# Another order of the mixer's projections: compressed keys, values and gates first, three query quarters last

## The chip, the cores and the metric

The kernel runs on one core of a Trainium2 chip. The metric is the device time of one launch in microseconds (us); lower is better. Before the change the median of three runs is 2270.88 us (2266.21 to 2273.49).

## The reference, cut to what matters

The program computes three transformer layers over 512 tokens of width 1024 in fp32. The change lies in the third layer, the mixer. It normalises x, projects it once with `w_in`, and splits the result:

```python
z = rms_norm_2(x, mix_norm_g) @ w_in
(nq, kc, vc, ks_, vs_, kw, vw, ng, cu, gq, gk, gv, ga, gr) = jnp.split(z, split_at, axis=-1)
kc, vc = compress_kv(kc, ...), compress_kv(vc, ...)       # blocks of 32 tokens through a small MLP
y_nsa  = nsa_attention(nq, kc, vc, ks_, vs_, kw, vw, sigmoid(ng), rel_bias)   # 8 heads of 64
y_conv = conformer_conv(cu, ...)                           # GLU, causal depthwise conv of 31, layer norm
o      = gla_chunked(gq, gk, gv, log_a)                    # 8 chunks of 64, a state carried from one to the next
y_gla  = rms_norm_2(o, ...) * silu(gr)
x = x + concatenate([y_nsa, y_conv, y_gla]) @ w_out
```

A feed-forward layer (called f2 below) follows.

## The kernel before

**Matmuls.** Every weight is split into a high and a low fp32r part (`weight`, line 370): a DMA on the SP queue into `wr` (2 buffers), a scaled copy on ACT into `wh`, a scaled difference on DVE into `wl` (4 buffers each). A product is then three fp32r matmuls (`mm3`, line 287). Line numbers of profile rows are mostly those of these helpers: 285 is every matmul, 295 every transpose, 148 every DVE, ACT or POOL instruction, so rows are told apart by tile.

**Order of work.** The program is written by Python threads (generators) that a small planner (`Order`, line 76) interleaves. Of the threads that can go on, the one with the lowest rank is taken; a thread yields a flag to wait for, or a time worked out from planned costs (`due`, `sleep`). Nothing of this exists on the chip: there the engines run their queues in order and wait on semaphores. The framework below may move an instruction ahead of its place where its operands and buffers are free.

**The mixer** (`mixer`, line 1378). One thread of rank 1, `project` (line 1505), runs ten projections in the order of the string `MIX_ORDER` (line 34):

- `conv`: 512 columns in two token halves; starts the 31-tap convolution (`conformer1`, rank 0, DVE), later `conformer2`.
- `b`: gla's values and gate ranks (400 columns, by token). `a`: attention's values and gates `gate`, and half of gla's output gate `gr` (408 columns, by token). When `a` ends, the flag `gates` is set.
- `gla`: gla's queries and keys (2 tiles of 128 columns); starts the thread `gla` (line 1752, rank 0). That thread waits for `gates` (line 1813) before it applies `gr`, then runs four token steps, each with two state updates (tiles `diag`, `gst`, `gA`, `gs`), and sets `done_c`.
- `k`: selected and window keys (2 tiles). `kv`: keys and values to be compressed (2 tiles); starts two `compress` threads (line 1603, rank 0) whose matmuls are `s<-Xp,w`.
- `q0` to `q3`: a quarter of the queries each (1 tile, two heads).

Each tile of 128 columns costs 8 x 3 matmuls of 512 columns. After the last projection the flag `made` is set. A thread `begin` (line 1511) waits for both compressions, the keys and `q0`, and sets `first`. Only then are the attention threads added: four of `lane` (line 1523, rank 0), for quarters t = 0 and 1 and their two heads e; each goes on with quarter t + 2. A lane waits for its own quarter `fq[t]` and, for t of 2 and 3, for `made`; the first lane of a quarter loads the bias tile `T` (`nsa_bias`, line 1589); then `nsa_c` scores the compressed keys (`s<-kch`), and `nsa` (line 1707) goes through four query tiles of growing length. When both heads of a quarter are done, the result is split into X, which needs `made`, since the projections read X.

Three threads of lower rank bring dense matmuls of 512 columns: `others` (line 1550, rank 1), which multiplies the conv and gla parts by `w_out` after `made`, `done_c` and `done_y`; `out(0)` after quarters 0 and 1; `out(1)` after quarters 2 and 3.

```python
MIX_ORDER = "conv b gla k q0 kv a q1 q2 q3"          # line 34
def begin():
    yield from self.wait(*cmp, ready, fq[0])
    first.done = True
```

Of the kernel before, what the change touches and what calls it, by code (L numbers as in the profile page):

```python
# [30 lines left out]
CONV_GAP = 1000.0  # L31
LAT = 200.0
FAC = 1.0
MIX_ORDER = "conv b gla k q0 kv a q1 q2 q3"
SL = 1.0
D = 1024
EPS = 1e-6
# [147 lines left out]
class Model:  # L185
# [1192 lines left out]
    def mixer(self, x, nxt):  # L1378
# [4 lines left out]
        with self.phase("mx") as pp:  # L1383
# [22 lines left out]
            made, done_c, done_v, done_y, done = fl(), fl(), fl(), fl(), fl()  # L1406
# [30 lines left out]
            fq, qs = [fl() for _ in range(4)], Slots(3)  # L1437

            def query(t):

                yield from (qs if t < 3 else self.xs).take()
                parts = [(lambda r, e=e: r.rearrange("p (k e d) -> p k e d", e=2, d=64)[:, :, e, :],
                          W[:, e * 256 + t * 64:e * 256 + t * 64 + 64].rearrange("(k p) d -> p k d", p=P))
                         for e in range(2)]
                yield from self.wu.take()
                units = [self.weight(1024, parts, [gm[:, k:k + 1] for k in range(8)])]

                qT[t] = (pp.tile([P, 2, S], F32R, name=self.uid("nq"), tag="nq", bufs=3) if t < 3 else
                         self.sc.tile([P, 2, S], F32R, name=self.uid("nq"), tag="xn"))
                yield from self.gemm_feat(x, units, P, [blk(0)], lambda j, ps: self.split_halves(qT[t], ps, 0.125))  # L1450
                fq[t].done = True

            with self.phase("mxc") as pc:
# [51 lines left out]
                def project():  # L1505
                    for job in MIX_ORDER.split():
                        yield from query(int(job[1])) if job[0] == "q" else {
                            "a": proj_a, "b": proj_b, "conv": proj_conv, "gla": proj_gla, "k": proj_k, "kv": proj_kv}[job]()
                    made.done = True
# [5 lines left out]
                ready, gates = fl(), fl()  # L1515
# [4 lines left out]
            with self.phase("mxn") as pn:  # L1520
                head, left, fy, fo = {}, [2] * 4, [fl() for _ in range(4)], [fl(), fl()]

                def lane(t0, e):
                    for t in (t0, t0 + 2):
                        yield from self.wait(fq[t], *([made] if t >= 2 else []))
                        if t not in head:
                            hd = head[t] = [fl()]
                            yield from heads.take()
                            yield from self.acc.take()
                            hd += [self.ptile("acc"), [], *self.nsa_bias(pn, t)]  # L1530
                            hd[0].done = True
                        yield from self.wait(head[t][0])
                        T2, cB = head[t][3:]
                        yield from self.cr.take()
                        yield from self.bank("s")
                        sc = self.nsa_c(pn, t, e, qT[t], kc, cB, gate)
                        ready = fl()
                        od.add(self.nsa_cv(sc, self.padded(vals[:, 8], e), head[t][1:3], ready), 0)
                        for qt in range(NT):
                            yield from self.nsa(pn, t, e, qt, qT[t], kh, kl, vals, T2, gate, head[t][1:3], ready)  # L1540
                        left[t] -= 1
                        if left[t] == 0:
                            (qs if t < 3 else self.xs).give()
                            heads.give()
                            yield from self.wait(made)
                            self.split(*[y[:, t, :] for y in self.X], head[t][1])
                            self.acc.give()
                            fy[t].done = True

                def others():  # L1550
                    yield from self.wait(made, done_c)
                    for t in range(NT):
                        ts = slice(t * P, (t + 1) * P)
                        yield from self.bank("tr")
                        self.split(*[y[:, 6:, ts] for y in self.X], self.transpose(gr[:, t, :], 2))
                        yield
                    yield from self.wait(done_y)
                    for c in range(2):
                        yield from self.gemm_tok(lambda k, t: self.x_at(4 + k, t), 4, [(Wo[512:, :], c * 512, 512)],
                                                 self.add_h(c * 512), lambda t: [])  # L1560
                    fo[0].done = True

                def unit(k0, m, pieces):
                    c0, parts = pieces[0][1], []
                    for e in range(2):
                        parts.append((lambda r, e=e: r.rearrange("p (a w) -> p a w", w=512)[e * 64:(e + 1) * 64],
                                      Wo[e * 256 + k0 * 64:e * 256 + (k0 + m) * 64, c0:c0 + 512]
                                      .rearrange("(a p) n -> p a n", p=64)))
                    return self.weight(m * 512, parts)

                def out(g):

                    yield from self.wait(*fy[2 * g:2 * g + 2], *fo[:g * 2])
                    token = nxt()[1] if g else lambda t: None
                    yield from self.gemm_rows(lambda k, t: self.x_at(2 * g + k, t), 2,
                                              lambda c, k0: unit(2 * g + k0, 2, [(Wo, c * 512, 512)]),
                                              lambda t: [], token)
                    (fo[1], done)[g].done = True

                self.nw, heads = Slots(2), Slots(2)  # L1580
                for t in range(2):
                    for e in range(2):
                        od.add(lane(t, e), 0)
                od.add(others(), 1)
                od.add(out(0), 2)
                od.add(out(1), 2)
                od.run(done)
# [397 lines left out]
```

## Time and profile before

| | |
|---|---|
| median of three runs | 2270.88 us (2266.21 to 2273.49) |
| the profiled execution's own time | 2270.06 us |
| its span from first to last instruction | 2268.3 us |
| mean granted TensorE clock | 0.988 of full speed |
| TensorE (PE) matmul busy | 2197.4 us, 97% |
| TensorE weight loads (PEld) | 1861.9 us, 82% |
| VectorE (DVE), ScalarE (ACT), GpSimd (POOL) | 1336.6, 1062.0, 173.0 us |
| the mixer's matmuls | from about 1534 to about 1831 us |

Times in the trace count from the span's start. The time of a launch is the span and about 2 us around it. Matmuls are pipelined and their ends are modelled, so that matmuls that come one by one can look like a busy engine: the number of starts in a stretch and the granted clock (1.00 is 2.4 GHz, 0.50 is 1.2 GHz) have to be read beside the busy time.

### The profile page before, as it was taken

Reading aid. Unit: us, or ns where it says so; the run is one execution under the profiler, and the core shown is the slowest. Engines: PE = TensorE matmul, PEld = TensorE weight load, DVE = VectorE, ACT = ScalarE, POOL = GpSimd, SP = SyncE. Lnnn points to the kernel's source line nnn. Section 1 sums busy time; section 2 is a strip of 40 time slices with the busy share of each in tenths; the row PEclk is TensorE's granted clock in tenths of the full one; section 3 lists DMA queues with packets and bytes.
Section 4 is the critical chain, followed back from the end, with each engine's and each line's share of the span. In section 5 each row is a group of like instructions: output and inputs, shape, how many; then the busy total and the mean of one; then the engine's idle time right before and its main releaser. Section 6 shows DMA issues by size and latency. Waiting matters only on the chain.

```text
span 2268.3 us, 30282 instructions
## 1 busy us (share of the span) xinstructions
PE 2197.4 (97%) x11166; PEld 1861.9 (82%) x11166; DVE 1336.6 (59%) x2885; ACT 1062.0 (47%) x2102; POOL 173.0 (8%) x232
## 2 busy tenths in 40 slices
PE   7987999999999999999999999999999999999998
PEld 5866798888887888888988888889978888888886
DVE  6668656446545777767565366357977643333344
ACT  4547445334444565555454254254657543323333
POOL 3123000000001121210000000001010000000000
PEclk9999999999999999999999999999989999999999
DMA  6323123332332412212133233234430123323322
GB/s 190 99 63 93 59 84 98 103 98 84 107 98 80 128 43 59 68 40 82 54 107 102 94 103 97 79 98 122 99 91 22 54 66 101 99 91 99 99 89 82
DMA packets 168839, 200.01 MB, mean 88 GB/s; under 512 B 19201, under 2 KB 123709, under 8 KB 168688
## 3 DMA queue, kind: packets, MB, share of 16 engines
q1 hardware_dynamic: 165172, 194.77, 28.1%
q10 hardware_dynamic: 2940, 2.02, 0.3%
q0 software_dynamic: 576, 1.26, 0.3%
q8 instruction: 88, 1.44, 0.3%
q14 instruction: 63, 0.52, 0.1%
HBM read 195.87 MB, written 7.38 MB: 90 GB/s over the span
## 4 chain that ended last, share of the span: by engine, by line
PE 91%; DVE 4%; ACT 1%; DMA 1%; issue 1%; POOL 0%; DVEq 0%; POOLq 0%; SPq 0%; ACTq 0%
PE acc L285 82%; PE s L285 4%; PE tr L295 4%; PE tr L285 1%; DVE wl L148 1%; DVE sb L148 1%; PE s L295 0%; DVE ss L148 0%; DVE X L148 0%; ACT wh L148 0%; DMA xn<-biasB 0%; DVE qs L148 0%; ACT wT L148 0%; DVE qn L148 0%; DMA tb<-rel_bias 0%
## 5 line engine op out<-in xcount | busy, mean ns | idle before, releaser
L285 PE MATMUL acc<-X,wh 128*128 128x512 f32 (+1 forms) x2592 | 734.9, 370 | 4.0 <-DVE X L148 4.0
L285 PEld LDWEIGHTS acc<-X,wh 128*128 128x128 f32 x2592 | 469.9, 189 | 85.0 <-DVE X L148 4.7
L285 PE MATMUL acc<-wh,X 128*128 128x512 f32 (+4 forms) x1664 | 502.0, 380 | 0.2 <-DVE X L148 0.2
L285 PE MATMUL acc<-X,wl 128*128 128x512 f32 (+1 forms) x1296 | 474.7, 369 | 0.0
L148 ACT ACTIVATE wh<-wr,gcol 128x512 fp32r<-128x512 f32 (+5 forms) x480 | 289.6, 656 | 208.4 <-PE acc L285 123.8
L148 DVE SCALAR_TENSOR_TENSOR wl<-wr,gcol,wh 128x512 fp32r<-128x512 f32 (+5 forms) x480 | 306.1, 674 | 131.5 <-ACT wh L148 129.5
L285 PEld LDWEIGHTS acc<-wh,X 128*128 128x128 f32 x1664 | 309.9, 190 | 45.9 <-DVE X L148 0.7
L285 PE MATMUL acc<-wl,X 128*128 128x512 f32 (+4 forms) x832 | 322.4, 388 | 7.3 <-DVE qn L148 3.3
L285 PEld LDWEIGHTS acc<-X,wl 128*128 128x128 f32 x1296 | 244.2, 189 | 40.8
L148 DVE TENSOR_TENSOR wl<-wr,wh 128x1024 fp32r<-128x1024 f32 (+1 forms) x134 | 152.5, 1144 | 183.8 <-ACT wh L148 183.6
L148 POOL TENSOR_TENSOR ss<-ss,mhalf 128x1 f32<-128x1 f32 (+3 forms) x140 | 128.9, 923 | 1727.4 <-DVE ss L148 1703.0
L148 ACT ACTIVATE wh<-wr 128x1024 fp32r<-128x1024 f32 (+1 forms) x134 | 132.5, 995 | 238.9 <-PE acc L285 191.2
L285 PE MATMUL acc<-wh,hh 128*128 128x512 f32 x528 | 205.7, 390 | 0.0
L285 PE MATMUL acc<-wl,hh 128*128 128x512 f32 x528 | 204.5, 389 | 0.0
L285 PE MATMUL acc<-wh,hl 128*128 128x512 f32 x528 | 203.7, 390 | 0.0
L285 PEld LDWEIGHTS acc<-wl,X 128*128 128x128 f32 x832 | 158.1, 190 | 32.8 <-DVE qn L148 3.6
L148 DVE SCALAR_TENSOR_TENSOR cv<-acc,cw,cv 128x511 f32<-128x511 f32 (+1 forms) x176 | 126.1, 745 | 95.2 <-ACT cv L148 94.4
L148 DVE TENSOR_TENSOR h<-h,acc 128x512 f32<-128x512 f32 x120 | 81.6, 684 | 61.3 <-PE acc L285 60.8
L285 PEld LDWEIGHTS acc<-wl,hh 128*128 128x128 f32 x528 | 99.1, 188 | 20.5
L285 PEld LDWEIGHTS acc<-wh,hl 128*128 128x128 f32 x528 | 99.1, 188 | 20.4
L285 PEld LDWEIGHTS acc<-wh,hh 128*128 128x128 f32 x528 | 99.1, 188 | 20.4
L148 ACT ACTIVATE wT<-tr 128x128 f32<-128x128 f32 (+3 forms) x160 | 68.8, 435 | 91.4 <-PE tr L295 90.6
(312 smaller groups left out, 2688.5 us busy)
## 6 DMA issues: line engine op xcount, KB each, us to landing
wr<-ffn_w_in SPq DMA_DIRECT2D x160, 256.0 KB
wr<-ffn_w_out SPq DMA_DIRECT2D x40, 512.0 KB
wr<-ple_w_gate SPq DMA_DIRECT2D x24, 512.0 KB
wr<-ffn_w_gate SPq DMA_DIRECT2D x40, 256.0 KB
wr<-ffn_w_up SPq DMA_DIRECT2D x40, 256.0 KB
wr<-ffn_w_down SPq DMA_DIRECT2D x20, 512.0 KB
wr<-a_w_qkv SPq DMA_DIRECT2D x32, 256.0 KB
wr<-b_w_o SPq DMA_DIRECT2D x16, 512.0 KB
```

Source lines behind the costliest of these rows:

```text
L148: return fn(*args, **kw)
L285: self.nc.tensor.matmul(out, lhsT=a, rhs=b, start=start, stop=stop)
L295: self.nc.tensor.transpose(out, src, self.ident[:src.shape[0], :src.shape[0]])
```

## The change

`MIX_ORDER` is another string, and a lane also waits for the flag `gates`. Nothing is added to or taken from what is computed.

```diff
-MIX_ORDER = "conv b gla k q0 kv a q1 q2 q3"
+MIX_ORDER = "conv kv a b k q0 gla q1 q2 q3"
...
                 def lane(t0, e):
                     for t in (t0, t0 + 2):
-                        yield from self.wait(fq[t], *([made] if t >= 2 else []))
+                        yield from self.wait(fq[t], gates, *([made] if t >= 2 else []))
```

## Rows read from the trace of the kernel before

**Rows 1.** Mixer by stretch: us, busy us and starts of PE PEld DVE ACT POOL, clock.
```profile
1562.00:1674.00 112.00, 112.00 (x618) 100.12 (x618) 98.18 (x199) 67.91 (x158) 5.97 (x11) 1.00 0.47 125
1674.00:1710.00 36.00, 32.09 (x157) 24.37 (x155) 29.38 (x137) 23.18 (x83) 2.61 (x4) 0.81 0.06 16
1710.00:1822.00 112.00, 111.19 (x751) 99.31 (x749) 73.33 (x262) 70.47 (x192) 1.61 (x2) 1.00 0.15 41
```

**Rows 2.** The same view and columns, shorter stretches.
```profile
1674.00:1684.00 10.00, 7.99 (x52) 6.71 (x51) 9.59 (x44) 8.16 (x24) 1.29 (x2) 0.94 0.21 53
1684.00:1698.00 14.00, 12.98 (x45) 9.44 (x43) 9.30 (x48) 5.00 (x20) 1.32 (x2) 0.56 0.00 1
1698.00:1710.00 12.00, 11.12 (x62) 8.22 (x62) 10.49 (x48) 10.02 (x40) 0.00 (x0) 1.00 0.00 1
1740.00:1750.00 10.00, 10.00 (x86) 9.73 (x86) 6.73 (x34) 7.58 (x23) 0.00 (x0) 1.00 0.00 0
1770.00:1780.00 10.00, 10.00 (x88) 9.82 (x87) 7.99 (x33) 6.78 (x20) 0.00 (x0) 1.00 0.01 2
```

**Rows 3.** Lanes by tile: min/median/max ns, first and last start.
```profile
L285 PE MATMUL s<-kch,nq x32: 178/263/1015, 1674.2 to 1778.8; 128*128 128x32 f32 x32
...
L285 PEld LDWEIGHTS s<-nkh,nq x64: 186/190/337, 1677.3 to 1812.5; 128*128 128x128 f32 x64
```

**Rows 4.** ACT in order of time, 1605 to 1680 us.
```profile
1622.05 0.59 ACT L148 ACTIVATE gk<-tr 64x512 f32<-64x512 f32 x1
...
1642.85 1.06 ACT L148 ACTIVATE gr<-gr 128x1024 f32<-128x1024 f32 x1
...
1671.62 0.58 ACT L148 ACTIVATE nq<-acc 64x512 fp32r<-64x512 f32 x1
```

**Rows 5.** Waits of PE, 1672 to 1712 us: total, times, longest.
```profile
PE acc L285 <- DVE gst L148: 1.5, 3, 0.9
...
PE s L285 <- DVE nm L148: 1.0, 2, 0.7
```

**Rows 6.** The gla thread by tile, the same columns.
```profile
L285 PE MATMUL acc<-gst,gq x16: 379/380/634, 1651.0 to 1707.7; 128*128 128x256 f32 x16
L148 ACT ACTIVATE gq<-acc x2: 379/382/384, 1581.9 to 1582.2; 128x256 f32<-128x256 f32 x2
...
L285 PE MATMUL tr<-diag,gs x8: 592/674/1201, 1650.1 to 1703.5; 128*128 128x512 f32 x8
```

**Rows 7.** Dense matmuls with `w_out`, by line, 1710 to 1822 us.
```profile
L285 PE MATMUL acc<-wh,X 128*128 128x512 f32 x102 | 32.9, 395 | 0.0
...
L285 PE MATMUL acc<-wl,X 128*128 128x512 f32 x51 | 21.0, 411 | 0.0
```

**Rows 8.** PE in order of time: dense matmuls of a query projection.
```profile
1667.92 0.62 PE L285 MATMUL acc<-X,wh 128*128 128x512 f32 x2
1668.37 0.39 PE L285 MATMUL acc<-X,wl 128*128 128x512 f32 x1
1668.60 0.62 PE L285 MATMUL acc<-X,wh 128*128 128x512 f32 x2
```

**Rows 9.** Compression, by tile.
```profile
L285 PE MATMUL s<-Xp,w x128: 215/275/275, 1627.9 to 1667.0; 128*128 128x62 f32 x128
```

**Rows 10.** Weight splits and table loads, by line, 1562 to 1710 us.
```profile
L148 DVE SCALAR_TENSOR_TENSOR wl<-wr,gcol,wh 128x256 fp32r<-128x256 f32 x24 | 10.4, 480 | 0.2 <-ACT wh L148 0.2
...
L148 DVE SCALAR_TENSOR_TENSOR wl<-wr,gcol,wh 128x128 fp32r<-128x128 f32 x32 | 9.4, 345 | 0.6 <-ACT wh L148 0.6
...
L148 ACT ACT_TABLE_LOAD x6 | 7.7, 1283 | 0.1
```

**Rows 11.** SP's queue in order of time; the bias tile's first readers, by tile.
```profile
1633.46 5.63 SPq L1630 DMA_DIRECT2D w<-cmp_w_v  x2
...
1665.49 1.10 SPq L1593 DMA_DIRECT2D T<-rowsC  x2
...
L148 DVE COPY cB<-T x16: 162/186/218, 1676.9 to 1753.3; 128x62 f32<-128x62 f32 x4, 128x46 f32<-128x46 f32 x4, 128x30 f32<-128x30 f32 x4, 128x14 f32<-128x14 f32 x4
```

## The prediction

> **What bounds the kernel now.** I read the page first: PE is nearly always busy and holds most of the chain of waits. No stretch can gain much, unless PE's busy time there is not what it seems. The next view, busy time by stretch, shows such a place. In the mixer's projections, from 1562 to 1674 us, PE is busy without a gap at full clock, although DVE is near its limit as well; from 1710 to 1822 us, attention beside the output projection, it is nearly so [rows 1]. In the 36 us between, PE is idle for 36 - 32.09 = 3.91 us, runs at a mean clock of 0.81, and starts 157 matmuls, 4.36 per us, where the stretch behind it starts 751 in 112 us, 6.71 per us [rows 1]. The shorter stretches show how: from 1674 to 1684 us PE works 7.99 of 10 us, and then the granted clock falls to a mean of 0.56 for 14 us, which is mostly the level of 1.2 GHz [rows 2].
>
> This is attention's start. The first lane scores start at 1674.2 us [rows 3]. The last query projection has just ended: its result is copied at 1671.62 us [rows 4]. So all four lanes start on their smallest tiles, where each matmul waits for a reduction or for gla's state update [rows 5], and no dense matmul is left to fill in: the `w_out` products wait for gla's end, and gla's last state matmul starts at 1707.7 us [rows 6]. Only behind 1710 us do 102 + 51 dense matmuls stand between attention's [rows 7]. Later stretches that hold hardly any of these, 1740 to 1750 and 1770 to 1780 us, have PE busy all the time at full clock [rows 2]: lanes on long tiles fill PE by themselves.
>
> **The change part by part.** *The recoverable loss.* Idle time is 3.91 us, the clock's loss is 36 x (1 - 0.81) = 6.84 us; together 10.75 us [rows 1]. Counted by starts, 157 matmuls at 6.71 per us are 23.4 us of work, so 12.6 us are lost; the mix differs, so I take 10.75 and keep 12.6 as the other end. The Trainium skill, Perfetto Trace Analysis, section Identifying the Most-Contended Engine, judges TensorE's headroom by the busy share of weight loads, not of matmuls. By that rule the stretch lacks 36 x 99.31 / 112 - 24.37 = 7.6 us [rows 1], and with the last term below the sum would be 2265.6 us, no change. The trace speaks against using it here: a load takes 190 ns at the median and up to 337 ns [rows 3], so at half clock the loads themselves are stretched, and their share hides the clock's part.
>
> *What moves behind attention's start.* In the new order `q0` is the last of the projections that `first` waits for; `gla` and `q1` to `q3` come after it. Three dense matmuls take from 1667.92 to 1668.60 us, 0.227 us each [rows 8]. Gla has 2 x 24 of them, 10.9 us, three queries 72, 16.3 us: 27.2 us of dense work leave the time ahead of the lanes and become fill between them. That is more than the 10.75 us lost, and it is there when the lanes are on their smallest tiles. The lanes then start at about 1674 - 27 = 1647 us, a little earlier still for gla's own matmuls. None of this work disappears; the gain is only that PE does it where it now stands still.
>
> *Compression* must be done by `q0`. Its matmuls now run from 1627.9 to 1667.0 us [rows 9], between 168 dense ones (`a`, `q1` to `q3`) without a loss on PE. After the change `a`, `b`, `k` and `q0`, 264 dense ones, follow `kv`: cost nothing. Without that cover the lanes would start later, but gla and the queries do not wait for `first` and would go on.
>
> *DVE.* The splits that move are 8 of 256 columns at 480 ns and 24 of 128 at 345 ns [rows 10], 12.1 us. DVE is busy 29.38 of the 36 us [rows 1]; with 12.1 more in some 36 - 11 + 27 = 52 us it is 80% busy, less than the 98.18 of 112 us that PE bears now [rows 1]. I take nothing; uncovered it would be up to 12.1 us.
>
> *SP and POOL.* Eight loads of weights go behind the first bias tiles in SP's queue, and `b`'s weights go behind loads of compression weights, which now block SP for 5.63 us [rows 11]. SP runs ahead of PE and PE shows no idle time then, so I take nothing; the upper end is 5.6 us. A bias tile that comes late costs at most the 11.4 us from its issue at 1665.49 to its first reader at 1676.9 us [rows 11], on lanes that have fill beside them: nothing. POOL is busy 2.61 of 36 us [rows 1]: nothing.
>
> *The new wait* on `gates` issues nothing. `a` precedes `q0`, so the flag is set before any lane is: nothing.
>
> *Gla late* is the price. Its queries are copied at 1581.9 us, its last state matmul starts at 1707.7 us [rows 6], 126 us; from 1622.6 to 1642.9 us it waits for `gates` [rows 4], which is now set beforehand. That leaves 106 us; its four steps alone take from 1650.1 to 1707.7 us, 58 us [rows 6]. Four lanes with gla use 4.36 / 6.71 = 65% of PE and leave 35% to fill; with two lanes, until `q1`, I take 65%, an estimate. Then gla's projection ends at 1647 + 10.9 / 0.65 = 1664 us, `q1` at 1672 us, and `q3` 10.9 / 0.35 = 31 us later, 1703 us. Gla ends between 1664 + 58 = 1722 and 1664 + 106 = 1770 us. In between lie 19 to 67 us, in the middle 43, in which lanes and gla are again without fill. The nearest row for this, lanes on middling tiles with gla at full clock, is 1698 to 1710 us: idle 0.88 of 12 us, 7.3% [rows 2]. So 43 us cost 3.1 us; at the loss of the whole start, 10.75 / 36 = 0.299 per us, 67 us would cost 20 us. I take 3.1, since by then quarter 0 and 1 are on long tiles.
>
> *Sum*, against the profiled execution's 2270.06 us (0.8 us below the median): 2270.06 - 10.75 + 3.1 = **2262.4 us**.
>
> **The rivals.** *The stall moves.* Fill is used up early, and when quarter 2 starts on small tiles without it, PE starves as before: 43 x 0.299 = 12.9 us given back, 2272.2 us, no change. For it: the planner gives fill whenever a lane waits, so it saves none for later. Against it: in the new order the quarters start some 25 us apart, so long tiles run beside short ones.
>
> *Gla late, slower.* If gla's chain stays at 106 us and the gap to `w_out` is 67 us, at 0.299 per us: 20.0 - 10.75 = 9.3 us more, 2279.4 us. It decides from (10.75 + 6.8) / 0.299 = 59 us of such a gap. For it: each gla step shares tile `diag` and DVE with the lanes. Against it: 1740 to 1750 us, where lanes alone fill PE [rows 2].
>
> *ACT's function tables.* The compressor's, gla's and conv's functions now alternate with the lanes' exponentials. ACT has six table loads at 1283 ns, 7.7 us, between 1562 and 1710 us [rows 10], nearly all before the lanes start. Six more in the lanes' chain would take 7.7 us back, 2270.1 us: no change. For it: gla's exponentials, logarithm and gate now run beside softmax. Against it: ACT is busy 67.91 of 112 us in the projections and 23.18 of 36 at the start [rows 1], and PE would have fill. The Trainium skill, ScalarE: Activation LUTs, section Rules for kernel authors, asks for just the opposite of such an order: all work of one table set before the next.
>
> *The change does nothing* in its second edit, as shown; the first cannot but move the work.
>
> **How the numbers follow.** About 0.3%, 6.8 us, is what a measurement of this kernel can tell from no change: faster is below 2264.1 us, slower above 2277.7 us. The forecast's mechanism has 0.56, of which 0.08 lies above 2264.1 us, since the gap to `w_out` is the weakest term. The moved stall has 0.18, the tables 0.09, gla late 0.17. Faster 0.48, same 0.08 + 0.18 + 0.09 = 0.35, slower 0.17. The low end is 2270.06 - 12.6 = 2257.5 us, and 2.5 us lower for a gap that costs nothing and lanes that end earlier beside dense work: 2255 us. The high end takes in both middle rivals and the uncovered DVE term (2274.5 us), and reaches to gla late, half of which lies beyond: 2279 us. The likeliest case by itself is 2257 to 2267 us.
>
> **What would show it.** Right: the first `s<-kch` near 1645 us; `gq` and `nq` copies behind it; the clock at 1.00 through attention's start; more starts per us there than 4.36; gla's last state matmul between 1722 and 1770 us; the mixer's end some 8 us earlier. Wrong: a stretch at half clock anywhere between 1640 and 1770 us, PE waiting for `wl` or for weights ahead of 1645 us, dense `w_out` work still unfinished when the lanes end and idle time before it, or more table loads with lanes waiting on ACT.

## The result, and the profile after

The change makes the kernel slower, by half a per cent: 2282.09 us median (2281.33 to 2285.3) against 2270.88 us, ratio 1.0056 with a 95% interval of 1.0039 to 1.0072. The profiled execution took 2281.78 us (span 2280.1 us, mean granted clock 0.988), 11.7 us more than the one before. 2262.4 us was forecast; the time lies above the range too, which ended at 2279 us.

To see what the mixer alone does, I take its length in the trace from the start of the program's 7400th matmul (1534.6 us before, in the first projection) to that of the 1500th from the end (1922.2 us before, in f2). All kernels here have 11,166 matmuls, so the points are the same work in each. Before it is 387.6 us, after 401.1 us: +13.5 us. (Of these, 1.8 us had been gained ahead of the mixer, so that the spans differ by 11.8 us.) The mixer's own length is used below beside the medians, as it leaves out what varies elsewhere. It comes from one execution of each kernel. Against the loss that the ratio of the medians gives (ratio minus 1, times 2270.88 us) it differs by up to 3 us over all the kernels below, so that a smaller difference between two of these lengths proves nothing by itself.

The busy time by stretch of the changed kernel, in the stretches of [rows 1] and with their columns:

```profile
1562.00:1674.00 112.00, 107.94 (x594) 96.80 (x593) 91.34 (x216) 58.76 (x145) 3.05 (x7) 0.97 0.43 116
1674.00:1710.00 36.00, 27.21 (x141) 21.56 (x139) 25.39 (x89) 29.59 (x76) 2.57 (x5) 0.81 0.10 33
1710.00:1822.00 112.00, 108.75 (x699) 95.08 (x700) 77.00 (x279) 64.96 (x198) 4.06 (x4) 0.98 0.08 20
```

All three are worse than in [rows 1]. The middle one, which the change was to repair, has 8.79 us idle in place of 3.91, and the same clock of 0.81. The other two were full, or nearly so, at clock 1.00. The same view of the changed kernel, divided where the lanes begin and where the dense work ends:

```profile
1640.00:1651.00 11.00, 6.94 (x35) 5.29 (x34) 9.69 (x48) 8.98 (x29) 0.90 (x2) 0.79 0.43 96
1651.00:1680.00 29.00, 29.00 (x142) 23.40 (x141) 15.38 (x47) 14.07 (x34) 2.03 (x4) 0.96 0.26 73
1680.00:1710.00 30.00, 21.21 (x107) 16.46 (x106) 20.78 (x69) 26.35 (x66) 1.65 (x3) 0.77 0.07 23
1710.00:1755.00 45.00, 41.79 (x291) 36.86 (x292) 35.53 (x150) 29.49 (x97) 3.06 (x3) 0.97 0.09 24
```

and of the kernel before:

```profile
1640.00:1651.00 11.00, 11.00 (x67) 9.44 (x66) 8.22 (x23) 7.92 (x19) 0.60 (x1) 1.00 0.84 234
1651.00:1680.00 29.00, 27.72 (x171) 23.68 (x169) 20.05 (x56) 16.91 (x44) 3.41 (x6) 1.00 0.45 129
1680.00:1710.00 30.00, 27.37 (x129) 20.76 (x128) 23.79 (x114) 17.36 (x68) 2.61 (x4) 0.77 0.00 1
1710.00:1755.00 45.00, 44.77 (x312) 40.03 (x311) 30.00 (x124) 30.56 (x87) 1.01 (x1) 1.00 0.09 25
```

Idle time plus the clock's loss (length times 1 minus the clock), over these 115 us: before 4.14 + 6.90 = 11.0 us, after 16.06 + 11.72 = 27.8 us. The difference of 16.8 us is 3.3 more than the mixer grew, since a busy matmul at half clock counts here as wholly lost; the places are what matters. There are three. From 1640 to 1651 us a stall that did not exist before (4.06 idle + 2.31 clock). From 1680 to 1710 us the old stall, with 8.79 us idle in place of 2.63. From 1710 to 1755 us a thin stretch (3.21 + 1.35), at whose end the clock falls a third time. In between, from 1651 to 1680 us, PE is full and VectorE and ScalarE are half idle: 15.38 and 14.07 of 29 us.

What happened there, by tile:

```profile
L285 PE MATMUL s<-kch,nq x32: 178/262/283, 1640.8 to 1757.8; 128*128 128x32 f32 x32
...
L148 ACT ACTIVATE gq<-acc x2: 378/382/385, 1642.5 to 1642.7; 128x256 f32<-128x256 f32 x2
...
L285 PE MATMUL acc<-gst,gq x16: 379/382/634, 1702.7 to 1762.5; 128*128 128x256 f32 x16
...
L285 PE MATMUL s<-Xp,w x128: 215/275/275, 1581.4 to 1608.0; 128*128 128x62 f32 x128
```

The lanes begin at 1640.8 us (1674.2 before), compression is over long before, and gla ends at 1762.5 us (1707.7 before). The dense matmuls of gla's second tile and of `q1` to `q3` (in the window from 1651 to 1680 us, by tile), and the dense `w_out` matmuls from 1710 to 1822 us, which answer to [rows 7]:

```profile
L285 PE MATMUL acc<-X,wh x64: 387/393/1415, 1651.1 to 1679.6; 128*128 128x512 f32 x64
...
L285 PE MATMUL acc<-X,wl x32: 387/389/577, 1652.7 to 1679.8; 128*128 128x512 f32 x32
...
L285 PE MATMUL acc<-wh,X 128*128 128x512 f32 x85 | 27.2, 394 | 0.0
L285 PE MATMUL acc<-wl,X 128*128 128x512 f32 x43 | 18.1, 421 | 0.0
```

All 96 dense matmuls are gone by 1679.8 us; the next (`w_out`) comes at 1755.4 us. They stand in TensorE's queue ahead of the lanes' next steps: in the tile view of `nsb` from 1640 to 1700 us the first scaled softmax is ready behind 1648.3 us, and its transpose starts at 1663.5 us, 15 us later, among dense matmuls.

```profile
L148 DVE TENSOR_SCALAR nsb<-nsb,z x12: 277/284/417, 1648.3 to 1698.2; 128x128 f32<-128x128 f32 x8, 128x256 f32<-128x256 f32 x2, 128x384 f32<-128x384 f32 x2
...
L295 PE MATMUL tr<-ident,nsb x11: 272/421/473, 1663.5 to 1699.6; 128*128 128x128 f32 x11
```

PE in order of time shows both stalls. The first one's longest wait is for VectorE's part (`nsc`) of a lane's start, and the first dense matmul stands behind a lane's `diag` step. The second one's longest wait is for gla's prologue, whose `tr<-U,gs` stands ahead of the lanes' transposes.

```profile
1644.63 0.25 PE L285 MATMUL s<-kch,nq 128*128 128x32 f32 x1 [2.54 <-DVE nsc L148]
...
1650.02 2.08 PE L285 MATMUL acc<-diag,vals 128*128 128x512 f32 x2 [1.24 <-ACT diag L148]
1651.10 1.84 PE L285 MATMUL acc<-X,wh 128*128 128x512 f32 x2
...
1688.49 2.05 PE L285 MATMUL tr<-U,gs 128*128 128x128 f32 x8 [3.94 <-DVE gs L148]
1690.33 0.64 PE L295 MATMUL tr<-ident,nsb 128*128 128x128 f32 x2
```

ScalarE is the busy engine at that point (26.35 of 30 us), with gla's, the conv's and the lanes' functions in turn:

```profile
1685.70 1.28 ACT L148 ACT_TABLE_LOAD   x1
1686.99 0.63 ACT L148 ACTIVATE gs<-gs 128x512 f32<-128x512 f32 x1
1687.64 1.28 ACT L148 ACT_TABLE_LOAD   x1
1688.93 1.06 ACT L148 ACTIVATE cy<-cy 128x1024 f32<-128x1024 f32 x1
...
1691.86 1.28 ACT L148 ACT_TABLE_LOAD   x1
```

### The profile page after: what moved, and what is told of

The parts are those of the page before. It is cut to its first block, busy times and chain, and to the rows that moved or that the text cites. A ratio compares the mean times of both kernels' runs of the same rounds, so it can differ in the third digit from the quotient of the medians.

```text
span 2280.1 us, 30264 instructions
## 1 busy us (share of the span) xinstructions
PE 2199.8 (96%) x11166; PEld 1863.2 (82%) x11166; DVE 1338.4 (59%) x2885; ACT 1061.5 (47%) x2103; POOL 173.3 (8%) x232
## 5 line engine op out<-in xcount | busy, mean ns | idle before, releaser
L148 ACT ACTIVATE cv<-acc,cw 128x512 f32<-128x512 f32 x88 | 66.0, 775 | 94.0 <-PE acc L285 94.0
```

The source lines that it names most:

```text
L148: return fn(*args, **kw)
```

## The experiments

The expectations name theories by letters. A: gla's late end leaves no `w_out` fill. B: the lanes' start and ScalarE's work stall PE's queue, whatever fill there is. C: two lanes starting alone make a stall of their own, and the moved dense work is spent before the main one. D: ScalarE's and VectorE's chains, table loads among them, stall the main start. E (last group): the kernels differ in how many bare stretches open, as each is followed by a time at half clock. All runs, with the mixer's length from each profiled execution; a ratio is to executions of the kernel before taken beside it, whose median lay between 2269.68 and 2270.88 us:

| kernel | median us | ratio to before | 95% interval | mixer us |
|---|---|---|---|---|
| before | 2270.88 | 1 | | 387.6 |
| after | 2282.09 | 1.0056 | 1.0039 to 1.0072 | 401.1 |
| e1_wout_free | 2280.27 | 1.0038 | 1.0024 to 1.0052 | 397.9 |
| e2_gla_before_k | 2277.22 | 1.0026 | 1.0018 to 1.0035 | 393.7 |
| e3_gla_late_alone | 2278.10 | 1.0032 | 1.0021 to 1.0044 | 393.9 |
| e4_kv_early_alone | 2273.60 | 1.0010 | 1.0000 to 1.0020 | 390.2 |
| e5_start_together | 2275.90 | 1.0024 | 1.0015 to 1.0033 | 394.0 |
| e6_conv_fill | 2267.77 | 0.9989 | 0.9980 to 0.9998 | 383.7 |
| e7_early_gla_hold | 2277.18 | 1.0027 | 1.0018 to 1.0036 | 394.1 |
| e8_hold_queries | 2281.74 | 1.0055 | 1.0040 to 1.0070 | 401.5 |
| e9_no_tables | 2279.66 | 1.0037 | 1.0023 to 1.0050 | 397.2 |
| e10_early_all_together | 2271.62 | 1.0006 | 0.9997 to 1.0015 | 388.3 |
| e11_two_queries_fill | 2269.82 | 0.9996 | 0.9987 to 1.0005 | 384.9 |
| e12_two_fill_conv | 2267.68 | 0.9991 | 0.9982 to 1.0000 | 384.1 |
| e13_fill_held | 2278.95 | 1.0039 | 1.0025 to 1.0053 | 393.5 |
| e14_held_conv | 2277.21 | 1.0032 | 1.0020 to 1.0044 | 394.1 |
| e15_fill_held_all | 2274.16 | 1.0015 | 1.0004 to 1.0025 | 392.4 |
| e16_hold_last_conv | 2268.30 | 0.9992 | 0.9983 to 1.0001 | 383.0 |
| e17_hold_last | 2270.76 | 1.0008 | 0.9999 to 1.0017 | 389.5 |
| e18_after_second_query | 2275.83 | 1.0028 | 1.0018 to 1.0039 | 394.5 |

### Is it gla's late end?

The changed kernel, with `w_out` not waiting for gla. It leaves out gla's finished result: the gla part of the output projection multiplies what gla has so far.

```diff
-                    yield from self.wait(made, done_c)
+                    yield from self.wait(made)
```

> The changed kernel, in which the thread of the dense w_out product for the conv and gla parts waits for the last projection only and no longer for gla's end (so the gla part of its input is the gate alone, without gla's result). Theory A (no fill: from the last query's projection, about 1684 us, to gla's end, about 1763 us, PE has no dense matmul beside the lanes): the idle time and clock loss of 1680 to 1755 us, some 20 us, mostly go, about 2265 us. Theory B (the lanes' start and ACT's work at 1680 to 1695 us, gla's first steps, conv's second part and three table loads, stall PE's queue in order, whatever fill there is): the stall before 1695 us stays and at most 4 us are gained, 2278 us or more.

Dense `w_out` work now starts at 1718.8 us. It also needs the conv's part of its input, which is written by 1694 us, and the gate's, by 1709 us; what held it from there on was not looked for. The stretch behind fills up, but the stall before it stays:

```profile
1680.00:1710.00 30.00, 21.07 (x99) 15.71 (x98) 20.68 (x72) 27.18 (x69) 2.57 (x5) 0.77 0.09 23
1710.00:1755.00 45.00, 44.85 (x319) 40.89 (x318) 32.67 (x129) 26.62 (x85) 2.27 (x2) 1.00 0.09 24
```

The mixer is 3.2 us shorter, the median 1.8, and the intervals of the two ratios overlap. The missing `w_out` fill from about 1719 us on is at most a small part of the loss. A as the main cause falls in so far as no `w_out` work comes in time for the stall even when it need not wait for gla; what it would do there, this run does not show.

### Which part of the order?

Three orders that do one part of the change each (only the string, and the wait on `gates`):

```diff
-MIX_ORDER = "conv kv a b k q0 gla q1 q2 q3"
+MIX_ORDER = "conv kv a b gla k q0 q1 q2 q3"      # e2
+MIX_ORDER = "conv b k q0 kv a gla q1 q2 q3"      # e3
+MIX_ORDER = "conv kv b gla k q0 a q1 q2 q3"      # e4
```

> The changed kernel with gla's projection two places earlier, ahead of k and q0: conv kv a b gla k q0 q1 q2 q3. The lanes start some 11 us later, gla some 20 us earlier, and only q1 to q3 are left as fill. Theory A: the gap without fill shrinks from about 72 to about 40 us, 2268 to 2273 us. Theory B: gla's first steps move ahead of the lanes and the stall at 1680 to 1695 us goes, about 2270 us; but the one at the lanes' start, 1640 to 1651 us, stays.

> The order of before with gla's projection alone moved, from the third place to behind a: conv b k q0 kv a gla q1 q2 q3. Theory A: the lanes start as before, about 1674 us, and gla ends some 40 us later, so the stretch without fill grows from 36 to about 75 us and the kernel becomes slower than before by about 10 us, 2281 us. Theory B: gla's first steps still lie ahead of the lanes, 2270 to 2275 us.

> The order of before with the compressed keys and values alone moved up, from the sixth to the second place: conv kv b gla k q0 a q1 q2 q3. Gla stays early, and the lanes start behind a with q1 to q3, 16.3 us of dense work, still to come. Theory A: gla ends before or soon after the queries do, so fill is there nearly all the time, 2260 to 2266 us, faster than before. Theory B: the lanes' start stalls PE as it did, 2268 to 2273 us.

None is faster than before, and none lies in the ranges that theories A and B gave it (e4 is 0.6 us above B's). With `gla` early (e4) most of the loss goes; with compression left late (e3) about half of the mixer's loss stays. But e2 has gla ahead of the lanes too and still loses 6 us of mixer time. So gla's place is not all of it. What all three and the changed kernel share is that the two lanes of quarter 0 are let go ahead of those of quarter 1 (they begin 11, 12, 16 and 30 us earlier; 8 us in the kernel before). Why e2 and e3 lose 6 us and e4 only 2.6 was not taken apart.

### The two starts

The changed kernel; the lanes wait for the last projection, so that all four start at once:

```diff
-                    yield from self.wait(*cmp, ready, fq[0])
+                    yield from self.wait(*cmp, ready, made)
```

> The changed kernel, but the attention lanes wait for the last projection instead of the first query quarter, so that all four start at once. Theory C (the change adds a second start stall of about 7.5 us from 1640 to 1651 us, where two lanes alone stand without dense work between their matmuls, and keeps the main one from 1680 to 1710 us because the moved dense work is spent before it as one lump): the early stall goes, one start remains, and gla is later against the lanes than before; 2275 to 2278 us, ratio 1.002 to 1.003. Theory A (only gla's late end and the missing w_out work cost time): gla ends no earlier, no gain, 2281 to 2283 us. Rival D (ScalarE's and VectorE's chains of gla and conv in the main start cost the time): they fall on four lanes' start, no gain or slower, 2282 us or more.

As theory C expected: 2275.90 us, mixer 7.1 us shorter, although the lanes begin 25 us later and all fill is gone before they do. The same stretches as above:

```profile
1640.00:1651.00 11.00, 11.00 (x52) 8.98 (x52) 8.81 (x26) 7.52 (x21) 1.14 (x2) 1.00 0.53 152
1651.00:1680.00 29.00, 26.77 (x132) 21.99 (x130) 19.46 (x66) 23.30 (x51) 3.06 (x6) 0.84 0.23 73
1680.00:1710.00 30.00, 24.14 (x117) 17.78 (x116) 22.94 (x89) 21.96 (x73) 2.42 (x3) 0.87 0.01 2
```

Waiting for `fq[1]` instead, with the other two quarters (10.9 us of dense work) behind the start, gives the same:

> The changed kernel, but the lanes wait for the second query quarter, so that all four start together with two quarters as fill; gla stays late. Theory E: one fall of the clock in place of two, as in the run in which the lanes waited for all projections, and 10.9 us of fill on top: 2272 to 2276 us. If the separate starts were not the cost: 2280 us or more.

2275.83 us. So letting quarter 0 go first costs 6.2 to 6.3 us of the changed kernel's median, and 10.9 us of fill brought nothing here. What shrinks is PE's idle time: over the mixer it is 20.2 us in the changed kernel, 13.1 in e5, 14.4 in e18. Theory E's one fall of the clock in place of two did not come: it falls near 1671 and 1684 us in e5, near 1674 and 1684 us in e18. Nor is it the distance alone that costs: the pairs still begin 12 us apart in e18 (1653.9, 1666.3 us) and 11 us apart in e11 below.

### What remains: gla, early compression, or the weights' order

Compression early, `gla` early, one start behind all projections:

```diff
-MIX_ORDER = "conv kv a b k q0 gla q1 q2 q3"
+MIX_ORDER = "conv kv b gla k a q0 q1 q2 q3"
...
-                    yield from self.wait(*cmp, ready, fq[0])
+                    yield from self.wait(*cmp, ready, made)
```

> Order conv kv b gla k a q0 q1 q2 q3, and the attention lanes start after the last projection, all four together. Compression is as early as in the changed kernel, gla is early as in the kernel before, and there is one start without fill. Theory C (the cost of the change is the second start, and gla beside the lanes' start and late): as the kernel before, 2269 to 2272 us. A theory by which early compression itself, or the order of the weights, costs time: 2274 us or more.

2271.62 us, no difference from before, mixer +0.7 us. The mixer's 13.5 us divide: 401.1 - 394.0 = 7.1 us for the separate starts, 394.0 - 388.3 = 5.7 us for gla's place (and `a`'s, which moves with it), 0.7 us for the rest of the order. By the medians the second term is 4.3 us.

The function tables, in the changed kernel. Left out are the logarithm in gla's decay (an exponential in its place) and the Silu of gla's gate and of the conv (copies):

```diff
-        nc.scalar.activation(la, la, AF.Ln, bias=1.0)
+        nc.scalar.activation(la, la, AF.Exp, scale=-1.0)
...
-        nc.scalar.activation(gr, gr, AF.Silu)
+        nc.scalar.activation(gr, gr, AF.Copy)
...
-        nc.scalar.activation(y, y, AF.Silu)
+        nc.scalar.activation(y, y, AF.Copy)
```

> The changed kernel, but the logarithm in gla's decay is an exponential, and the last activations (Silu) of gla's gate and of the conv are copies: these functions are left out, so that ScalarE need load no other function table while the lanes run. Rival D (ScalarE's table loads and chain in the stretch from 1680 to 1710 us stall attention's main start): three loads of 1.28 us go, 3.8 us, and what waits behind them; 2276 to 2279 us. Theory C (dense work is missing there, whatever ScalarE does): 2280 to 2283 us.

The three loads at 1685.70, 1687.64 and 1691.86 us are gone; the mixer is 3.9 us shorter, about three loads of 1.28 us. The median falls by 2.4 us, but the intervals of the two ratios overlap, so the gain is not shown. Nor need it be the loads' own time: the fall of the clock in that stretch is also shorter (mean 0.89 for 0.77, 3.6 of its 30 us). PE's wait for `gs` is shorter and not gone:

```profile
1680.00:1710.00 30.00, 22.52 (x125) 17.43 (x124) 23.82 (x84) 24.63 (x70) 2.60 (x5) 0.89 0.08 23
...
1688.67 2.05 PE L285 MATMUL tr<-U,gs 128*128 128x128 f32 x8 [2.64 <-DVE gs L148]
```

D is a part of the loss at most, and not the whole. Table loads elsewhere cost nothing that can be seen: e10 has nine between 1562 and 1710 us, before has six.

### Does dense work behind the start help at all?

The kernel before, with its own order, but the conv part of `w_out` (48 dense matmuls) as a thread that need not wait for gla:

```diff
+                def others_conv():
+                    yield from self.wait(made, done_y)
+                    for c in range(2):
+                        yield from self.gemm_tok(lambda k, t: self.x_at(4 + k, t), 2, [(Wo[512:768, :], c * 512, 512)],
+                                                 self.add_h(c * 512), lambda t: [], tail=1)
+                    fc.done = True
...
```

> The kernel before, with its order, but the output projection's conv part is a thread of its own that need not wait for gla: 2 x 4 groups of 6 dense matmuls (48, 10.9 us) come free at about 1680 us, in the middle of attention's start, for 8 more additions on VectorE (0.7 us each). The premise of the prediction (dense work beside the start recovers the 10.75 us lost there): 2262 to 2266 us. Theory C, in-order queue: dense matmuls that stand ahead of the lanes' next steps as a lump delay them as much as they fill; 2268 to 2272 us. Rival D (VectorE and ScalarE bound the start): the 8 additions make it longer, 2271 to 2276 us.

Stretches of this run, beside [rows 1] and [rows 2]:

```profile
1674.00:1710.00 36.00, 33.23 (x184) 26.63 (x182) 32.14 (x122) 22.56 (x74) 3.21 (x6) 1.00 0.20 54
1710.00:1822.00 112.00, 108.68 (x745) 96.04 (x745) 78.41 (x288) 72.71 (x209) 1.61 (x2) 1.00 0.10 32
...
1680.00:1685.00 5.00, 4.07 (x28) 3.65 (x29) 4.75 (x20) 4.55 (x12) 0.00 (x0) 1.00 0.10 21
1685.00:1690.00 5.00, 5.00 (x30) 4.35 (x30) 4.92 (x27) 1.95 (x8) 1.27 (x2) 1.00 0.02 3
1690.00:1695.00 5.00, 5.00 (x24) 3.88 (x23) 4.77 (x14) 1.25 (x2) 0.00 (x0) 1.00 0.00 0
1695.00:1700.00 5.00, 5.00 (x32) 4.38 (x30) 4.86 (x20) 1.26 (x5) 0.00 (x0) 1.00 0.43 105
```

The fall of the clock is gone, with the first `w_out` matmul at 1682.5 us. Here the premise held for the clock. The gain is 3.9 us of mixer time (median 2267.77 us, ratio 0.9989, the interval just below 1), not 10.75, and the time lies between the ranges of the premise and of theory C. Two things are left: PE is still idle for 2.77 us of the 36 (3.91 before), and from 1710 to 1822 us, where these 48 matmuls are now missing, for 3.32 us (0.81 before).

Then the premise in the order of e10, with the lanes waiting for `fq[1]` (e11), and the same with the conv thread (e12):

> As the run before it in this list, but the lanes start after the second query quarter, so that all four start together while two quarters, 48 dense matmuls of 10.9 us, are still to come. The prediction's premise in its cleanest form (dense work behind the start fills the idle time and keeps the clock up): some 6 to 9 us of the start's loss are recovered, 2262 to 2266 us. Theory C, with TensorE's queue in order (the dense matmuls are put ahead of the lanes' next steps in one lump, and the lanes wait behind them): the start's stall comes after the lump, 2268 to 2273 us.

> As the run before it, and the output projection's conv part is a thread of its own that need not wait for gla (48 more dense matmuls that come free at about 1680 us; 8 more additions on VectorE of 0.7 us). If fill that comes free late, when the lanes already wait, is what helps: 2264 to 2268 us, below both kernels. If fill taken from later is missed there: 2268 to 2271 us.

e11: the mixer is 3.4 us shorter than e10's, the median 1.8 us lower, and neither differs from before by the bound of 0.3%. That is theory C's range, not the premise's. The dense matmuls end at 1679.3 us, and the stall follows at once:

```profile
1675.00:1680.00 5.00, 5.00 (x29) 4.17 (x28) 4.77 (x14) 2.75 (x8) 0.55 (x1) 1.00 0.35 101
1680.00:1685.00 5.00, 3.31 (x20) 2.15 (x17) 4.17 (x15) 4.94 (x9) 0.00 (x0) 1.00 0.06 19
1685.00:1690.00 5.00, 4.32 (x18) 3.81 (x17) 3.09 (x8) 4.72 (x11) 0.00 (x0) 0.58 0.31 90
1690.00:1695.00 5.00, 3.49 (x11) 2.14 (x11) 4.67 (x23) 2.97 (x13) 1.27 (x2) 0.50 0.01 3
```

e12 has 2267.68 us, the same as e6 within the intervals: twice the fill, no more gain.

### Can the fill be kept for the stall?

First by a flag in the planner: quarters 2 and 3 wait until all four lanes have had their compressed scores emitted, in the changed kernel (e8) and in the order of e4 (e7).

```diff
                 if t >= 2:
+                    yield from self.wait(all4)
```

> The changed kernel, but the projections of query quarters 2 and 3 wait until all four lanes of quarters 0 and 1 have had their compressed scores emitted, so that 48 dense matmuls (10.9 us) are kept for the second pair's start. Theory C (the fill was spent before the second pair's start): the second pair starts beside dense matmuls and the stretch from 1680 to 1710 us loses some 6 of its 15.8 us; 2274 to 2277 us. Theory A (gla's late end): no change, 2281 to 2283 us. Rival D (chains of ScalarE and VectorE stall the lanes, whatever TensorE has beside them): the fill is done there but the lanes end no earlier, 2280 to 2283 us.

> The order conv kv b gla k q0 a q1 q2 q3 (gla ends early) with quarters 2 and 3 of the queries held until all four lanes have started. Against the same order without holding (2273.6 us). Theory C: the main start gets 48 dense matmuls as fill and loses some 5 us; 2266 to 2270 us, below both kernels. Theory A: gla is early in both, no change, 2272 to 2275 us. Rival D: 2272 to 2276 us.

e8 says nothing about the theories: the dense matmuls end at 1678.3 us on the chip, no later than without the flag (1679.8). The flag orders the program's text only, and the framework may move an instruction ahead of its place. In e7 quarter 3 alone came later (copied at 1701.4 us), and it is 3.6 us slower than e4, where theory C expected it to be faster.

So the hold was made with data: a one-column copy on VectorE from a lane's softmax into the projection's PSUM tile, on top of e11, for quarters 2 and 3 after two and four lanes (e13), with the conv thread (e14), and both after four lanes (e15):

```diff
+                if hold:
+                    self.nc.vector.tensor_copy(ps[:, :1], self.soft[:, 0, :1])
```

> The kernel with all four lanes starting after the second query quarter, in which the 48 dense matmuls of quarters 2 and 3 are now held by data: a one-column copy on VectorE from a lane's softmax into the projection's PSUM tile, for quarter 2 when two lanes, for quarter 3 when all four lanes have emitted their first softmax. Two copies of about 0.15 us are added. Theory C (the fill was in TensorE's queue ahead of the stall, and was spent before it): the dense matmuls now fall between 1675 and 1700 us and recover some 5 us more than without the hold, 2263 to 2267 us. The other reading (the stall is VectorE's and ScalarE's chain, which the projections' own copies lengthen): 2269 to 2274 us.

> The same with the output projection's conv part as a thread of its own. If fill in the stall is what is scarce, 48 further dense matmuls help little, since the stall is already filled: 2262 to 2267 us, no more than 2 us from the run before it. If both leave later stretches without fill: 2267 to 2270 us.

> As the first run of this list, but both quarters are held until all four lanes have emitted their first softmax. Theory C: the fill falls later still, as a lump of 10.9 us; 2264 to 2268 us. The other reading: 2269 to 2274 us.

Theory C falls here in its second half: fill that is held back is worse, 2278.95, 2277.21 and 2274.16 us (e14, with the conv thread, is the second) against 2269.82 for e11 and 2267.68 for e12. The stretches of e13, whose two copies run at 1674.29 and 1693.07 us, show why:

```profile
1665.00:1670.00 5.00, 2.80 (x11) 2.03 (x11) 4.80 (x22) 3.28 (x10) 1.26 (x2) 0.50 0.30 107
1670.00:1675.00 5.00, 4.68 (x23) 4.42 (x22) 4.57 (x28) 3.55 (x14) 0.79 (x2) 0.50 0.00 0
1675.00:1680.00 5.00, 5.00 (x18) 4.05 (x18) 1.75 (x10) 4.06 (x6) 0.00 (x0) 0.68 0.00 0
1680.00:1685.00 5.00, 5.00 (x23) 3.88 (x22) 2.16 (x7) 0.94 (x1) 0.00 (x0) 1.00 0.00 0
1685.00:1690.00 5.00, 3.64 (x20) 2.73 (x19) 4.63 (x13) 3.93 (x14) 0.87 (x2) 0.84 0.42 103
1690.00:1695.00 5.00, 4.46 (x11) 3.04 (x12) 5.00 (x30) 3.56 (x13) 0.41 (x1) 0.50 0.01 2
```

Now two bare stretches open, ahead of the held work and between its two parts, and each has its fall to 0.50. PE does not sit idle before the held matmuls themselves (none of their groups has idle time before it), so it is not at the hold that PE's queue stands still. Last, only quarter 3 held, after two lanes (e17), and with the conv thread (e16):

> All four lanes start after the second query quarter, the third quarter is free, and the fourth alone is held by data until two lanes have emitted their first softmax. Theory E (what counts is that no stretch of a few us without dense work opens while the lanes are on small tiles: each one costs its idle time and is followed by some 8 to 16 us at half clock, one such fall in the kernel before, two in the changed kernel and in the runs with both quarters held): with 24 matmuls directly behind the start and 24 later the fall comes later or is shorter, 2266 to 2270 us; if a gap opens ahead of the held quarter there are two falls, 2272 to 2276 us. A reading by which only the amount of fill counts: 2269 to 2271 us, as without the hold.

> The same with the output projection's conv part as a thread of its own, which comes free at about 1685 us. Theory E: dense work lies in three parts from the start to about 1705 us, no fall of the clock or a short one, 2263 to 2267 us. By the amount of fill alone: 2267 to 2269 us, as without the hold.

e17 has two falls again (0.51 at 1670 us, 0.66 at 1690 us) and a mixer 4.6 us longer than e11's, but its median is only 0.9 us higher and the intervals of their ratios overlap: no difference is shown. e16 has one short fall and no less time than e12. Both times lie where the amount of fill alone puts them and not where theory E does. Place, not amount, decides between e11, e13 and e15, which all have the same 48 matmuls behind the start; no placement tried kept the clock up through the whole start but e6's.

Of all versions e6 is the one to take: 0.1% below the kernel before, a gain at the edge of what was measured. e12 and e16 have the same time and a larger edit.

## Why the prediction was wrong

**What bounds the kernel now** was read rightly: the 36 us from 1674 to 1710 were the weak stretch, and e6 shows that dense work there removes the fall of the clock. Only "each matmul waits" is too strong: the waits of [rows 5] are five, 2.5 of the 3.91 us.

**The step that failed** is "27.2 us of dense work leave the time ahead of the lanes and become fill between them ... and it is there when the lanes are on their smallest tiles". I compared amounts, 27.2 against 10.75 us, and not places. Gla's first tile was done ahead of the lanes; the other 96 matmuls (21.8 us at 0.227 us) went between 1651.1 and 1679.8 us, 76% of PE's time, where I had assumed 65% and then 35%. So the last query ended at 1680 us and not at 1703. None lay in the first lanes' first 10 us, none in the stretch where the four lanes together are on small tiles. That stretch moved by some 6 us and grew. Moreover the lanes of quarter 0 and 1 now start 30 us apart (1640.8, 1671.3 us), so that there are two starts; that quarters "start some 25 us apart" I had counted in the change's favour. It cost 7.1 us of the mixer's 13.5 (e5).

**The recoverable loss** was also mis-sized. Where the fill did lie right (e6), 3.9 us came back of 10.75. The clock's term, 6.84 us, went to nothing; of the 3.91 us of idle time 2.77 stayed; and 2.5 us of new idle time came in the stretch from which the fill was taken. A clock's loss counted as length times 1 minus the clock is also an upper bound, since it takes a busy matmul at half clock as wholly lost.

**Gla late.** The bounds held: its end at 1762.5 us lies within 1722 to 1770. The gap without dense work was 75.6 us (1679.8 to 1755.4), not 43, and lost 0.27 us per us (idle 8.79 + 3.21 and clock 6.90 + 1.35 us), not 7.3%: nearly the 0.299 of the start, which I had set aside "since by then quarter 0 and 1 are on long tiles". In its first 30 us, which lost 52%, that was not so: at 1680 us quarter 1 was on its first query tile and quarter 0 on its third. The 45 us behind lost 10%, not far from 7.3%. The rival "Gla late, slower" forecast 2279.4 us and comes nearest, its gap too short by 9 us. But its mechanism, the `w_out` fill that comes late, is worth 3.2 us at most as far as e1 could test it; gla's place, with `a`'s, costs 5.7 us where all lanes start together (e5 against e10). That this comes from its prologue beside the lanes' start is what PE's wait for `gs` suggests; of that only the functions were tried (e9). So the cause of this part stays open.

**The stall moves** is the rival that names the mechanism: fill used up early, starving later. I priced it as a repetition of the old stall on quarter 2 and so as no change; it came on quarters 0 and 1, and twice.

**ACT's tables**: three loads in the lanes' chain, not six; without them the mixer is 3.9 us shorter (e9), within the 7.7 us priced, and the medians do not show a gain. The Trainium skill, ScalarE: Activation LUTs, section Rules for kernel authors, asks for one set's work before the next; e9 agrees in direction, and no run shows it clear of noise. Its section What ACT_TABLE_LOAD costs gives 1283 ns and a drain of about 1380 ns more; the rows agree with the first, and show no gap for the second (a load at 1685.70 us, the next activation at 1686.99, the one ahead of the load ending at 1685.69).

**Right**: the lanes' start (1640.8 us against 1647 "a little earlier still"), in part by luck: only 21.8 of the 27.2 us went behind it, and with the 1.8 us gained ahead of the mixer that explains 23.6 of the 33.4 us; some 10 us are other work, gla's steps among it, which I had called a little. Right too that compression, VectorE's splits, SP, POOL and the wait on `gates` cost nothing: e10 has compression early, the weights in nearly the new order, the wait on `gates`, and no difference from before.

## What to carry to other kernels

Work moved behind a stall fills it only if it stands in the engine's queue between the instructions that stall. Count what the queue gives it, and write down when it will be used up, before its amount is held against the loss. Let chains that start on small tiles go together, if no dense work stands beside the first of them: here letting two of four lanes go first cost 6 us. And fill moved from elsewhere is a loan; price the place that it is taken from.

## What was not expected of the hardware

A bare stretch costs more than its idle time. In every run but e6, attention's start, where PE's idle time in 5 us reaches 1.3 us (before) to 4.0 us (e1), has one or more falls of the clock to 0.50, the 1.2 GHz level, each for some 3 to 17 us in which PE is mostly busy: in the kernel before 14 us at a mean of 0.56 with 1.02 us idle [rows 2]; in e13 twice within 30 us. In e6, idle for 0.93 us of one such stretch with dense work behind it, the clock stayed at 1.00. Nor is each bare stretch followed by a fall, as theory E has it: in e3, where PE is idle for 2.41 of the 5 us from 1690 us on, the clock stays at 1.00 to the mixer's end.

```profile
1690.00:1695.00 5.00, 2.59 (x15) 1.72 (x14) 4.91 (x13) 2.30 (x8) 0.00 (x0) 1.00 0.17 57
1695.00:1740.00 45.00, 41.92 (x267) 33.42 (x266) 36.44 (x141) 29.90 (x104) 4.18 (x4) 1.00 0.07 18
```

The clock's part in 1640 to 1755 us was 6.9 us before and 11.7 after, which has two falls more, near 1646 and 1752 us. The Trainium skill, TensorE: Matmul & The Clock Gate, section HAM oscillation (how this bites in real kernels), describes a kernel of short bursts whose clock falls at each wait; these rows agree in part, as falls come at waits here, but not at each. Why some short gaps bring a fall and others don't was not tried.
